# Narrow streams for every product, and a 64-byte lead in the tiles of the normed input

## The chip, the core and the metric

The kernel runs on one core of one Trainium2 chip. The metric is the device time of one execution in microseconds; of the kernel before there are three such times, with a median of 687.1 us. One further execution was taken by the hardware profiler, and everything said of single instructions comes from it. In the profile PE is TensorE's matmul stream and PEld its weight loads, DVE is VectorE, ACT ScalarE, POOL GpSimd, and SP the engine that issues the loads and stores.

## What is computed

Two pre-norm residual layers over 256 tokens of 2048 channels in float32: one of multi-head latent attention (16 heads), one of sliding-window grouped-query attention with sinks (32 query heads, 4 key/value heads), each gated, and a last norm.

```python
for i in range(DEPTH):                      # 2
    h = rmsnorm(x, layer_norm[i])
    if i % 2 == 0:                          # c_q, c_kv, k_rope, gate = split(h @ w_in)
        y, gate = mla_mixer(h, positions, ...)
    else:                                   # q, k, v, gate = split(h @ w_in)
        y, gate = swa_mixer(h, positions, ...)
    x = x + (y * jax.nn.silu(gate)) @ w_out
return rmsnorm(x, final_norm)
```

## The kernel before

The residual stream stays transposed, channels on partitions and the 256 tokens along the free axis, in 16 chunks of 128 channels. A float32 product runs as float32r passes over exact halves: a value is hi + lo, and hi*hi + hi*lo + lo*hi are summed in PSUM. A tile of the normed input (hs, one per chunk of channels) or of the gated mixer output (ys, the same) is [128, 2, 256], the hi half beside the lo half, 2048 bytes a partition. Both families come from the pool const, which hands out tiles one behind the other.

The weights (class Weights, L49 to L96) come in pieces of 128 x 1024. A load on the SP queue fills a raw tile; ACT copies it to the hi half (L89) and DVE subtracts for the lo half (L90). Five raw buffers and four of each half rotate, loads run three pieces ahead of the splits and the splits two ahead of the products. Each piece feeds eight chunks of channels.

`slab` (L254) is the inner product for one piece: half of the channels, for one chunk of 128 outputs. It has two forms. The wide form takes two matmuls a chunk of channels: the lo weights with the 256 hi columns (L266, L269), and the hi weights with all 512 columns of the tile, hi and lo beside each other (L267). Its PSUM bank then holds two sums, which are added afterwards: by `whole` (L271: an ACT copy at L274, a DVE add at L275), or by a second DVE add into the residual (L585, L732). The narrow form (`proj`, L247) takes three matmuls of 256 columns (L250, L251, L252), all into the same 256 columns of PSUM.

The wide form serves layer 0's gates (L551), both output projections (L583, L730) and layer 1's keys (L593); the narrow form layer 1's queries and gates (L635, L646). The latents at the start, the products that bring the latents up to heads (`up`, L453) and the values are narrow in any case.

Program order on each engine is the order in which the code issues. In layer 0, for each of eight pairs of heads: the query's two heads (L482), the previous pair's mix of the values (L466 to L469, whose last product is in plain float32), the query's rope part, the key, the value (L536 to L538), then four gate slabs, with the scores behind the first (L560 to L568) and the float32 transposes of the probabilities (L358, L359) behind the third. In layer 1, for each chunk c: a query half, the transposes, the next scores (L659 to L662), the other query half, a gate half, the values' products (L685, 512 columns wide, and L687), the other gate half. The last two output chunks of layer 1 have a form of their own (L739 to L757).

Of the kernel before, what the change touches and what calls it, by code (L numbers as in the profile page):

```python
"""One MLA layer and one sliding-window GQA layer with sinks, gated, pre-norm, on one core.

The residual stream stays transposed ([channel, token]) from the first load to the last store, so
every projection's result is already the next product's moving operand. Float32 products run as
three float32r passes over exact 12-bit halves (hi*hi + hi*lo + lo*hi, float32 sums in PSUM).
The per-token scale of a norm commutes with the projection behind it and is applied to its result.
"""
# [36 lines left out]
WARM = 2  # L44
MASK_MLA = [(i + 16) % 32 for i in range(32)]
# [3 lines left out]
class Weights:  # L49
    """The weights in the order of use: loads run ahead of the splits, the splits of the products."""  # L50
# [9 lines left out]
    def add(self, ap, width, step=SUB, beside=0):  # L60
        """beside: the halves alternate by that many columns, over the two tiles."""
        for at in range(0, width, step):
            n = min(step, width - at)
            self.pieces.append((ap[:, at:at + n], n, beside))
# [35 lines left out]
def trunk(ctx: ExitStack, tc: tile.TileContext, a: dict):  # L100
# [36 lines left out]
    # the functions' table, before it is waited for  # L137
# [23 lines left out]
    ident = const.tile([P, P], F32, name="ident")  # L161
    make_identity(nc, ident)
    # sums the partitions' two halves, into both
# [9 lines left out]
    # key block | query block: full causal [0 | diag], and window [strictly above | diag]  # L173
# [11 lines left out]
    hs = [const.tile([P, 2, S], F32R, name=f"hs{c}") for c in range(KC)]  # L185
    ys = [const.tile([P, 2, S], F32R, name=f"ys{c}") for c in range(KC)]

# [4 lines left out]
    def split(dst, src):  # L192
        """dst[:, 0] + dst[:, 1] = src, exactly."""
        act.copy(out=dst[:, 0, :], in_=src)
        dve.tensor_tensor(out=dst[:, 1, :], in0=src, in1=dst[:, 0, :].bitcast(F32), op=ALU.subtract)  # L195

    def split_scaled(dst, src, col):
        """The same of src * col, a scale per partition."""
# [4 lines left out]
    class Squares:  # L203
        """The sum over channel chunks of squares, as [128, token]; the rest of the sum is PE's."""
# [14 lines left out]
        def total(self, t):  # L219
            """The sums as a [128 tokens, 2] column, in four columns of a PSUM tile."""  # L220
# [4 lines left out]
    def rsqrt(name, tot, n, times=None):  # L225
        """(tot / n * times ** 2 + eps) ** -0.5 of [128 tokens, 2] columns."""
# [11 lines left out]
    def row(name, col, t):  # L238
        """A [128 tokens, 2] column as a row over the tokens, in every partition; by way of PSUM."""
# [7 lines left out]
    def proj(ps, lhs, rhs, first, last):  # L247
        """ps[n, token] += w.T @ h for one chunk of 128 channels: three passes."""
# [5 lines left out]
    def slab(ps, half, src, wide=True):  # L254
        """ps[n, token] += w.T @ src for half of the channels. Wide: the moving halves share a pass,
        and ps[:, S:] holds the sum with src's lower half."""
        hi, lo = w.next()
        k0 = half * (KC // 2)
        for k in range(k0, k0 + KC // 2):
            n = slice((k - k0) * P, (k - k0 + 1) * P)  # L260
            first, last = k == 0, k == KC - 1
            if not wide:
                proj(ps[:, 0:S], (hi[:, n], lo[:, n]), src[k], first, last)
                continue
            if not first:
                mm(ps[:, 0:S], lhsT=lo[:, n], rhs=src[k][:, 0, :], start=False, stop=False)  # L266
            mm(ps, lhsT=hi[:, n], rhs=src[k].rearrange("p a q -> p (a q)"), start=first, stop=last)  # L267
            if first:
                mm(ps[:, 0:S], lhsT=lo[:, n], rhs=src[k][:, 0, :], start=False, stop=False)  # L269

    def whole(ps):  # L271
        """The sum of a wide pass's two halves."""
        t = work.tile([P, S], F32, tag="wb", name="wb", bufs=1)
        act.copy(out=t, in_=ps[:, S:])  # L274
        dve.tensor_tensor(out=t, in0=ps[:, 0:S], in1=t, op=ALU.add)  # L275
        return t
# [10 lines left out]
    def rope_tables(name, i, pos_f):  # L287
        """cos and signed sin of positions * freq, the angle brought to [-pi, pi]."""
# [25 lines left out]
    def stack_pair(dst, src):  # L314
        """dst[:, 0] = [hi; lo] of src's upper 64 rows, dst[:, 1] = [lo; hi] of its lower 64."""
# [5 lines left out]
    def stack_same(dhi, dlo, src, r):  # L321
        """dhi = [hi; hi], dlo = [lo; lo] of 64 rows of src."""
# [6 lines left out]
    def softmax(ps, j, nm, sm, mask, scale, sink):  # L329
        """exp of one head's scores; -max and the sums, in columns by query block and head of the pair."""  # L330
# [21 lines left out]
    def turn(pair, both):  # L352
        """The pair's probabilities with the keys on partitions, split: key block 0 by head and
        query, then key block 1 by head, for the last queries (there whole, unless both)."""
# [17 lines left out]
    def silu(ps, rB):  # L372
        """silu of a gate chunk: x/2 * (1 + tanh(x/2)), x = ps * rB."""
# [8 lines left out]
    # ================= layer 0 =================  # L382
    # the latents, channel chunk by channel chunk as x arrives: eight output chunks at a time
# [12 lines left out]
    # two output chunks share a bank and one accumulation, which zeros open (and warm the clock)  # L396
# [80 lines left out]
    for g in range(HEADS // 2):  # L477
# [70 lines left out]
        for step in range(4):  # L548
# [3 lines left out]
            if step % 2 == 1:  # L552
                sgs.append(silu(whole(ps), r0B))
# [318 lines left out]
```

## Time and profile before

| | |
|---|---|
| three timed runs | 687.06, 687.10, 687.69 us |
| the profiled execution, first to last instruction | 687.5 us |
| matmuls on PE | 4918 |
| wide matmuls of `slab` (L267) | 480 with ys, 288 with hs |
| narrow passes with hs into pp (L250, L251, L252) | 572 each |
| memory traffic | 113.95 MB read, 2.10 MB written |

The profiled execution's span lies between the fastest and the slowest timed run, so what lies around the span is smaller than what these figures resolve. Stages, by where their first instructions stand: the latents up to about 50 us, layer 0's pairs of heads to 259, its output projection to 349.5, layer 1's keys and values to 373, its loop over chunks to about 590, its output projection to 664, the last two chunks and the final norm to the end.

A window of the profile gives, for a stretch of time, the busy time of each engine with the number of instructions that touch the stretch, the granted TensorE clock (1.00 is full), the DMA engines' share and the rate moved. A group gives line, engine, operation, output and inputs, shapes and count, then the busy time and the mean of one in ns, then the idle time ahead of them and what ended it. Matmuls overlap, and their ends are modelled.

### The profile page before, as it was taken

The page shows a single profiled execution, that of the slowest core. Times are in us where ns is not written, and L with a number is a line of the kernel's source. Part 1 is how long each engine was busy: PE and PEld are TensorE (multiplying, and loading weights), DVE is VectorE, ACT ScalarE, POOL GpSimd, SP SyncE. Part 2 cuts the span into 40 slices and gives each one's busy share as a digit, 9 for nine tenths or more (in the row PEclk, how much of TensorE's full clock was granted, in tenths as well). Part 3 has the DMA queues.
Part 4 walks back from the last instruction along what each step waited for, and adds up shares of the span by engine and source line. Part 5 has one row for each costly group of instructions (what it writes and reads, how often), then busy time and mean ns, then how long its engine had stood idle before and what let it go on. Part 6 is the DMA issues. An engine that isn't in the chain of part 4 may idle for free.

```text
span 687.5 us, 13007 instructions
## 1 busy us (share of the span) xinstructions
PE 672.9 (98%) x4918; PEld 632.1 (92%) x4918; DVE 554.2 (81%) x1133; ACT 435.2 (63%) x871; POOL 64.6 (9%) x72
## 2 busy tenths in 40 slices
PE   8999999999999999999999999999999999999994
PEld 7999899999999998888889999999999999888894
DVE  5887887787788786777768899999998998777764
ACT  6666666766666665444446688787788788444430
POOL 3624000000000000111110000000000000022220
PEclk9999999999999999999999999999999999999997
DMA  8664444554554555555555544544545444555504
GB/s 310 246 217 157 154 157 152 184 161 147 163 166 162 158 180 164 193 186 193 182 185 158 181 157 155 177 155 156 169 146 176 159 151 154 178 190 184 184 32 123
DMA packets 37296, 116.89 MB, mean 170 GB/s; under 512 B 4209, under 2 KB 8945, under 8 KB 37233
## 3 DMA queue, kind: packets, MB, share of 16 engines
q1 hardware_dynamic: 37232, 116.06, 51.6%
q8 instruction: 38, 0.62, 0.4%
q14 instruction: 26, 0.20, 0.1%
HBM read 113.95 MB, written 2.10 MB: 169 GB/s over the span
## 4 chain that ended last, share of the span: by engine, by line
PE 89%; DVE 3%; ACT 3%; POOL 2%; issue 1%; DMA 1%; SPq 0%; DVEq 0%; ACTq 0%; POOLq 0%
PE pp L267 26%; PE pp L266 12%; PE pp L252 11%; PE pp L251 11%; PE pp L250 11%; PE pt L358 2%; ACT whi L89 1%; PE pp L751 1%; PE yp L685 1%; PE pp L537 1%; PE pp L538 1%; PE pp L536 1%; DMA wraw<-in_w_c 1%; DVE wlo L90 1%; PE pp L269 1%
## 5 line engine op out<-in xcount | busy, mean ns | idle before, releaser
L89 ACT CAST whi<-wraw 128x1024 fp32r<-128x1024 f32 (+1 forms) x217 | 223.3, 1030 | 162.7 <-PE pp L267 88.4
L90 DVE TENSOR_TENSOR wlo<-wraw,whi 128x1024 fp32r<-128x1024 f32 (+1 forms) x217 | 260.4, 1202 | 60.8 <-ACT whi L89 58.7
L267 PE MATMUL pp<-ys,whi 128*128 128x512 f32 x480 | 167.7, 397 | 0.0
L252 PE MATMUL pp<-hs,wlo 128*128 128x256 f32 x572 | 159.7, 280 | 1.3 <-DVE wlo L90 1.2
L251 PE MATMUL pp<-hs,whi 128*128 128x256 f32 x572 | 159.6, 279 | 0.5 <-DVE hs L200 0.5
L250 PE MATMUL pp<-hs,whi 128*128 128x256 f32 x572 | 159.5, 279 | 0.2 <-ACT whi L89 0.2
L266 PE MATMUL pp<-ys,wlo 128*128 128x256 f32 x450 | 126.3, 281 | 0.0
L251 PEld LDWEIGHTS pp<-hs,whi 128*128 128x128 f32 x572 | 108.3, 189 | 0.9 <-DVE hs L200 0.9
L252 PEld LDWEIGHTS pp<-hs,wlo 128*128 128x128 f32 x572 | 107.4, 188 | 1.9 <-DVE wlo L90 1.9
L250 PEld LDWEIGHTS pp<-hs,whi 128*128 128x128 f32 x572 | 107.6, 188 | 0.4 <-ACT whi L89 0.4
L216 POOL TENSOR_TENSOR sq_x<-sq_x,sq 128x256 f32<-128x256 f32 x43 | 51.6, 1199 | 581.5 <-ACT sq L215 339.9
L267 PEld LDWEIGHTS pp<-ys,whi 128*128 128x128 f32 x480 | 88.4, 188 | 19.4 <-DVE ys L195 0.2
L267 PE MATMUL pp<-hs,whi 128*128 128x512 f32 x288 | 102.7, 397 | 0.0
L266 PEld LDWEIGHTS pp<-ys,wlo 128*128 128x128 f32 x450 | 84.5, 188 | 1.4
L266 PE MATMUL pp<-hs,wlo 128*128 128x256 f32 x270 | 76.4, 283 | 0.0
L267 PEld LDWEIGHTS pp<-hs,whi 128*128 128x128 f32 x288 | 53.6, 188 | 10.4
L266 PEld LDWEIGHTS pp<-hs,wlo 128*128 128x128 f32 x270 | 50.7, 188 | 0.8
L344 ACT ACTIVATE p<-p,nm 128x128 f32<-128x128 f32 x96 | 42.9, 448 | 12.4 <-DVE nm L340 12.4
L250 PE MATMUL pp<-cq,whi 128*128 128x256 f32 x96 | 27.5, 287 | 0.0
L252 PE MATMUL pp<-cq,wlo 128*128 128x256 f32 x96 | 26.9, 280 | 0.0
L251 PE MATMUL pp<-cq,whi 128*128 128x256 f32 x96 | 26.9, 280 | 0.0
L200 DVE SCALAR_TENSOR_TENSOR hs<-x,gains,hs 128x256 fp32r<-128x256 f32 x32 | 25.0, 792 | 2.1 <-ACT hs L199 2.1
(255 smaller groups left out, 1223.2 us busy)
## 6 DMA issues: line engine op xcount, KB each, us to landing
wraw<-in_w_g SPq DMA_DIRECT2D x64, 512.0 KB, 3.6
wraw<-in_w_o SPq DMA_DIRECT2D x64, 512.0 KB, 3.4
wraw<-in_w_q SPq DMA_DIRECT2D x32, 512.0 KB, 3.6
wraw<-in_w_ukv SPq DMA_DIRECT2D x16, 512.0 KB, 3.6
wraw<-in_w_c SPq DMA_DIRECT2D x15, 512.0 KB, 7.1
wraw<-in_w_uq SPq DMA_DIRECT2D x8, 512.0 KB, 3.6
wraw<-in_w_uq SPq DMA_DIRECT2D x8, 256.0 KB, 2.7
wraw<-in_w_k SPq DMA_DIRECT2D x4, 512.0 KB, 3.3
```

Of the source, the lines that this page charges most:

```text
L89: self.nc.scalar.copy(out=hi, in_=src)
L90: self.nc.vector.tensor_tensor(out=lo, in0=src, in1=hi.bitcast(F32), op=ALU.subtract)
L200: dve.scalar_tensor_tensor(out=dst[:, 1, :], in0=src, scalar=col, in1=dst[:, 0, :].bitcast(F32), op0=ALU.mult, op1=ALU.subtract)
L216: pool.tensor_tensor(out=self.acc, in0=self.acc, in1=t, op=ALU.add)
L250: mm(ps, lhsT=wh, rhs=rhs[:, 0, :], start=first, stop=False)
L251: mm(ps, lhsT=wh, rhs=rhs[:, 1, :], start=False, stop=False)
L252: mm(ps, lhsT=wl, rhs=rhs[:, 0, :], start=False, stop=last)
L266: mm(ps[:, 0:S], lhsT=lo[:, n], rhs=src[k][:, 0, :], start=False, stop=False)
L267: mm(ps, lhsT=hi[:, n], rhs=src[k].rearrange("p a q -> p (a q)"), start=first, stop=last)
L269: mm(ps[:, 0:S], lhsT=lo[:, n], rhs=src[k][:, 0, :], start=False, stop=False)
L344: act.activation(out=p[:, cols], in_=p[:, cols], func=AF.Exp, scale=-1.0, bias=nm[:, c:c + 1], accum_out=sm[:, c:c + 1])
L358: nc.tensor.transpose(t[:, 0, j * S + i * P:j * S + (i + 1) * P], p[:, i * P:(i + 1) * P], ident)
```

## The change

Four edits, and no other (comments and docstrings also go, which moves the line numbers).

1. `slab` keeps only its narrow form; `whole` goes, and so do the second adds into the residual.
2. The values' products of layer 1 with the first key block take two matmuls of 256 columns in place of one of 512.
3. Each hs tile is allocated 16 elements (64 bytes) longer, and its data begin behind these 16. A tile then takes 2112 bytes, so the data of tile c move by 64(c + 1) bytes, and every tile that const and the pools behind it hand out later moves by 1024.
4. Nothing is done to ys, whose tiles keep their form.

```diff
+OFF = 16
...
-    hs = [const.tile([P, 2, S], F32R, name=f"hs{c}") for c in range(KC)]
+    def offset(name):
+        t = const.tile([P, OFF + 2 * S], F32R, name=name)
+        return t[:, OFF:].rearrange("p (a q) -> p a q", a=2)
+
+    hs = [offset(f"hs{c}") for c in range(KC)]
     ys = [const.tile([P, 2, S], F32R, name=f"ys{c}") for c in range(KC)]
...
-    def slab(ps, half, src, wide=True):
+    def slab(ps, half, src):
         hi, lo = w.next()
         k0 = half * (KC // 2)
         for k in range(k0, k0 + KC // 2):
             n = slice((k - k0) * P, (k - k0 + 1) * P)
-            first, last = k == 0, k == KC - 1
-            if not wide:
-                proj(ps[:, 0:S], (hi[:, n], lo[:, n]), src[k], first, last)
-                continue
-            if not first:
-                mm(ps[:, 0:S], lhsT=lo[:, n], rhs=src[k][:, 0, :], start=False, stop=False)
-            mm(ps, lhsT=hi[:, n], rhs=src[k].rearrange("p a q -> p (a q)"), start=first, stop=last)
-            if first:
-                mm(ps[:, 0:S], lhsT=lo[:, n], rhs=src[k][:, 0, :], start=False, stop=False)
-
-    def whole(ps):
-        t = work.tile([P, S], F32, tag="wb", name="wb", bufs=1)
-        act.copy(out=t, in_=ps[:, S:])
-        dve.tensor_tensor(out=t, in0=ps[:, 0:S], in1=t, op=ALU.add)
-        return t
+            proj(ps[:, 0:S], (hi[:, n], lo[:, n]), src[k], k == 0, k == KC - 1)
...
-                sgs.append(silu(whole(ps), r0B))
+                sgs.append(silu(ps[:, 0:S], r0B))
...
         dve.tensor_tensor(out=xc(c), in0=ps[:, 0:S], in1=xc(c), op=ALU.add)
-        dve.tensor_tensor(out=xc(c), in0=ps[:, S:], in1=xc(c), op=ALU.add)
...
-        rope(kf1, whole(kps[c]), cos1R, sin1R, MASK_SWA)
+        rope(kf1, kps[c][:, 0:S], cos1R, sin1R, MASK_SWA)
...
         for n, p in enumerate(pt):
-            mm(yp, lhsT=v0, rhs=p[:, 0:4 * P], start=n == 0, stop=False)
+            for j in range(2):
+                o = slice(j * S, (j + 1) * S)
+                mm(yp[:, o], lhsT=v0, rhs=p[:, o], start=n == 0 and j == 0, stop=False)
```

Two places of PE's order show it. The first is where layer 0 ends: the last pair's mix of the values (yp), and the first chunks of channels of the output projection (pp, from ys). Before:

```order
L468 MATMUL yp<-ptl,vh 128x256
L469 MATMUL yp<-pt_3410,v_3280 128x128
L267 MATMUL pp<-ys_151,whi 128x512
L269 MATMUL pp<-ys_151,wlo 128x256
L266 MATMUL pp<-ys_152,wlo 128x256
L267 MATMUL pp<-ys_152,whi 128x512
L266 MATMUL pp<-ys_153,wlo 128x256
L267 MATMUL pp<-ys_153,whi 128x512
```

Now, with the changed kernel's line numbers (L256 to L258 are `proj`):

```order
L458 MATMUL yp<-ptl,vh 128x256
L459 MATMUL yp<-pt_3613,v_3462 128x128
L256 MATMUL pp<-ys_151,whi 128x256
L257 MATMUL pp<-ys_151,whi 128x256
L258 MATMUL pp<-ys_151,wlo 128x256
L256 MATMUL pp<-ys_152,whi 128x256
L257 MATMUL pp<-ys_152,whi 128x256
L258 MATMUL pp<-ys_152,wlo 128x256
```

Each chunk of channels has three matmuls in place of two, the hi weights come ahead of the lo weights in all of them, and the first slab follows the float32 product directly in both.

The second place is layer 1's loop, between a chunk's two gate halves: the values' products (yp, from the turned probabilities pth and ptl and the values vs). Before:

```order
L252 MATMUL pp<-hs_142,wlo 128x256
L685 MATMUL yp<-pth,vs_4437 128x512
L685 MATMUL yp<-ptl,vs_4437 128x512
L687 MATMUL yp<-pth,vs_4438 128x2x128
L687 MATMUL yp<-ptl,vs_4438 128x2x128
L250 MATMUL pp<-hs_143,whi 128x256
```

Now:

```order
L258 MATMUL pp<-hs_142,wlo 128x256
L676 MATMUL yp<-pth,vs_4911 128x256 x2
L676 MATMUL yp<-ptl,vs_4911 128x256 x2
L678 MATMUL yp<-pth,vs_4912 128x2x128
L678 MATMUL yp<-ptl,vs_4912 128x2x128
L256 MATMUL pp<-hs_143,whi 128x256
```

The gate's passes stand as they did; two products of 512 columns have become four of 256.

More of the change, by code (lines that the diff above doesn't have):

```diff
@@ L634, in query @@
         ps = bank(ps_p, "pp")
-        slab(ps, 0, hs, False)
+        slab(ps, 0, hs)
         yield
-        slab(ps, 1, hs, False)
+        slab(ps, 1, hs)
         qf = work.tile([P, S], F32, tag="ro3", name="ro3")
@@ L645, in gate @@
         ps = bank(ps_p, "pp")
-        slab(ps, 0, hs, False)
+        slab(ps, 0, hs)
         yield
-        slab(ps, 1, hs, False)
+        slab(ps, 1, hs)
         sg_of[c] = silu(ps[:, 0:S], r1B)
@@ L731, in trunk @@
         dve.tensor_tensor(out=xc(c), in0=ps[:, 0:S], in1=xc(c), op=ALU.add)
-        dve.tensor_tensor(out=xc(c), in0=ps[:, S:], in1=xc(c), op=ALU.add)
         sq_x2.add(xc(c))
```

## The prediction

> **What bounds the kernel now.** I read the page's busy time first, then its chain, then its costliest groups.
>
> ```profile
> PE 672.9 (98%) x4918; PEld 632.1 (92%) x4918; DVE 554.2 (81%) x1133; ACT 435.2 (63%) x871; POOL 64.6 (9%) x72
> PE 89%; DVE 3%; ACT 3%; POOL 2%; issue 1%; DMA 1%; SPq 0%; DVEq 0%; ACTq 0%; POOLq 0%
> ...
> L89 ACT CAST whi<-wraw 128x1024 fp32r<-128x1024 f32 (+1 forms) x217 | 223.3, 1030 | 162.7 <-PE pp L267 88.4
> L267 PE MATMUL pp<-ys,whi 128*128 128x512 f32 x480 | 167.7, 397 | 0.0
> L252 PE MATMUL pp<-hs,wlo 128*128 128x256 f32 x572 | 159.7, 280 | 1.3 <-DVE wlo L90 1.2
> ```
>
> PE is busy for 98% of the span and holds 89% of the chain. The weights' splits wait for PE (162.7 us idle before L89, 88.4 of it until L267 releases a buffer), not PE for them: L267 has no idle time, L252 1.3 us. So TensorE's own pace sets the time, and the question is what one streamed column costs. The mean of one matmul does not say it, because a matmul's end is modelled and overlaps the next one's start. I therefore took stretches that begin with the first pass of a slab (eight channel chunks) and end where the next work starts:
>
> ```profile
> core 0: us, PE busy (x), PEclk, DMA share, GB/s
> 91.29:94.01 2.72, 2.72 (x27) 1.00 0.46 142
> 405.79:408.51 2.72, 2.72 (x27) 1.00 0.50 178
> 85.92:88.75 2.83, 2.83 (x25) 1.00 0.57 185
> 409.20:412.02 2.82, 2.82 (x26) 1.00 0.54 186
> 104.23:107.05 2.82, 2.82 (x18) 1.00 0.47 166
> 276.19:281.83 5.64, 5.64 (x33) 1.00 0.58 190
> ...
> 395.37:408.51 13.14, 13.14 (x115) 1.00 0.49 161
> ```
>
> (The x counts up to three neighbours whose ends reach in.) In order: the key's two heads from ck, 24 narrow passes; layer 1's first gate half, 24; the query's two heads from cq, 24; the second gate half of the same chunk, 24; a layer 0 gate slab, 8 wide pairs; an output chunk of layer 0, two slabs of 8 wide pairs; and one whole round of layer 1's loop. Every slab streams 24 x 256 = 6144 columns, wide or narrow, and the granted clock is 1.00 in all. Yet there are two paces: 2.72 us (113 ns for 256 columns) and 2.82 us (117.5 ns). The wide slabs show the slow one; the narrow ones show both, with identical instructions:
>
> ```profile
> L252 PE MATMUL pp<-hs,wlo 128*128 128x256 f32 x9 | 2.5, 276 | 0.0
> L251 PE MATMUL pp<-hs,whi 128*128 128x256 f32 x9 | 2.5, 276 | 0.0
> L250 PE MATMUL pp<-hs,whi 128*128 128x256 f32 x8 | 2.2, 276 | 0.0
> ...
> L251 PE MATMUL pp<-hs,whi 128*128 128x256 f32 x8 | 2.2, 281 | 0.0
> L252 PE MATMUL pp<-hs,wlo 128*128 128x256 f32 x8 | 2.2, 281 | 0.0
> L250 PE MATMUL pp<-hs,whi 128*128 128x256 f32 x8 | 2.2, 281 | 0.0
> ```
>
> These are the two gate halves, 405.80 to 408.48 and 409.21 to 412.00: 276 ns a pass in the one, 281 in the other. Between them stand the values' products, two of them 512 wide. So I read two **rhythms**, and a narrow slab keeps the one it enters with. What leaves a narrow slab in the fast one is a fresh start at the first pass of a channel chunk, as behind the values' float32 product in layer 0:
>
> ```profile
> 89.68 0.38 PE L469 MATMUL yp<-pt,v 128*128 128x128 f32 x2
> 89.82 0.36 PE L250 MATMUL pp<-cq,whi 128*128 128x256 f32 x1
> 90.02 0.28 PE L251 MATMUL pp<-cq,whi 128*128 128x256 f32 x1
> ...
> 90.61 0.28 PE L250 MATMUL pp<-cq,whi 128*128 128x256 f32 x1
> 90.72 0.28 PE L251 MATMUL pp<-cq,whi 128*128 128x256 f32 x1
> 90.83 0.28 PE L252 MATMUL pp<-cq,wlo 128*128 128x256 f32 x1
> 90.95 0.28 PE L250 MATMUL pp<-cq,whi 128*128 128x256 f32 x1
> ```
>
> From 90.61 to 90.95 three passes take 0.34 us, and the key behind them (91.29 above) goes on at 2.72 until the next wide slab.
>
> **The change, part by part.** The span is 687.5 against a median of 687.1: I sum against the span and take 0.4 off at the end.
>
> Narrow in place of wide: 768 pairs become triples of the same columns. The slabs are 32 in layer 0's output projection, 28 in layer 1's (its last two chunks are as before), 32 gate slabs of layer 0 and 4 of layer 1's keys: 96. At the slow rhythm nothing is won; at the fast one each wins 2.82 - 2.72 = 0.10, together 9.6 us. The entries speak for the fast one: layer 0's output projection now follows the same float32 product as the row at 89.82, and two of a group's four gate slabs follow the narrow value products or the float32 transposes.
>
> Values in halves: the four half products stream the same columns, and nothing 512 wide stands in layer 1's loop any more. If it was this that upset the rhythm, the second gate half and the query half after it go from 2.82 to 2.72: 14 chunks x 2 x 0.10 = 2.8 us.
>
> The query's two heads in layer 0 (85.92, at 2.83) follow a gate slab that is no longer wide: 7 groups x 0.11 = 0.8 us.
>
> Given back: after a restart a few passes run slow (90.02 to 90.61 is 0.59 us for five, 0.02 more than at the fast rhythm). At most four times a group in layer 0's gates, that is 32 x 0.02 = 0.6 us.
>
> The Trainium skill's page "TensorE: Matmul & The Clock Gate" (Back-to-back issue gap) speaks against the change: each matmul costs its columns at 2.4 GHz and about 2.5 ns, so 768 more matmuls would cost 1.9 us and no slab would be won. Here 256 columns take 113 or 117.5 ns, not the 109 of that rule, so I do not sum by it.
>
> ACT and DVE lose work:
>
> ```profile
> L274 ACT COPY wb<-pp x18: 352/374/375, 80.3 to 364.8; 128x256 f32<-128x256 f32 x18
> L275 DVE TENSOR_TENSOR wb<-pp,wb x18: 418/425/426, 80.7 to 365.5; 128x256 f32<-128x256 f32 x18
> L585 DVE TENSOR_TENSOR x<-pp,x x16: 424/424/425, 265.6 to 350.2; 128x256 f32<-128x256 f32 x16
> ...
> 393.00:577.00 184.00, 184.00 (x1569) 182.85 (x1568) 170.33 (x439) 143.84 (x337) 0.00 (x0) 1.00 0.49 161
> ```
>
> Eighteen foldings and 30 second adds go, about 27 us of busy time. (The last row's pairs are PE, PEld, DVE, ACT and POOL in layer 1's loop.) All of it lies under PE, which is not seen idle in the stages concerned, so I cost it at nothing; a gain of up to half a microsecond at layer 1's start is not counted. What is late next is DVE in layer 1's loop: 170.33 of 184.00 us. There no DVE work goes, and PE's loop would shrink by 2.8 to 181.2, still 11 us above DVE's.
>
> The offset: an hs tile grows from 2048 to 2112 bytes a partition, so tile c's data moves by 64(c + 1) bytes while weights and ys all move by 1024. Against a weight slice (a multiple of 512 bytes into its tile), the odd tiles keep their distance modulo 128 and the even ones shift by 64. No long run of such passes is in the trace. 2400 passes stream hs in the slabs (768 layer 0 gates, 96 keys, 1536 queries and gates), half of them from even tiles. The nearest rows are single passes at which stream and weights change their tiles:
>
> ```profile
> L252 PE MATMUL pp<-cq,wlo 128*128 128x256 f32 x1 | 0.3, 285 | 0.0
> L250 PE MATMUL pp<-hs,whi 128*128 128x256 f32 x1 | 0.3, 286 | 0.0
> ```
>
> The first is the last query pass before the mix (88.6), the second layer 1's first query pass (372.98); they take 9 to 10 ns more than 276. From below, no narrow row is under 276, so I allow no gain beyond the fast rhythm except as a small chance. So the even passes cost 0 to 1200 x 9 = 10.8 us. I take 0, since 276 is also what hs, cq and ck passes show in whole slabs. The Trainium skill's page "SBUF — State Buffer" (Who interferes with whom) says the same: TensorE's two read ports are independent and wait for nobody, which makes the offset worth 0; that two rhythms exist at one clock shows that something else is missing from it.
>
> Sum: 9.6 + 2.8 + 0.8 - 0.6 = 12.6 us; 687.5 - 12.6 = 674.9, and less 0.4 it is **674.5**.
>
> **The rivals.**
> *The shifted tiles hold half of the passes back.* If the even tiles' passes run at the slow rhythm, 1200 x 4.2 ns = 5.0 us come back: 679.5. For it: the distance is all that differs. Against: the rows above show no tie between distance and rhythm.
> *All hs slabs fall into the slow rhythm*, since every second tile upsets it: 2400 x 4.2 = 10.1 us back, 684.6. Only ys gains.
> *The rhythm is not the width's doing.* Wide or narrow, everything stays as it is; the extra matmul of a triple then costs what separates two slow narrow slabs (2.82 and 2.83) from a wide chunk (5.64): 0.01 us in 16 channel chunks, 0.5 us in 768. 687.6. Against it: the row at 89.82 and the gate halves. By the 2.5 ns of the Trainium skill's page "TensorE: Matmul & The Clock Gate" (Back-to-back issue gap) it would be 689.0.
> *Slower: the even tiles collide with the weight load.* Each even pass pays the 9 ns of the 285 row, and the odd passes behind them the slow rhythm's 4.2: 1200 x 9 + 1200 x 4.2 = 15.8 us, 690.3. It decides from 12.6 / 2400 = 5.3 ns a pass on, just above the slow rhythm.
> *The even tiles stream better* than any row shows, by as much as the two known rhythms lie apart: 1200 x 4.2 = 5.0 us more, 669.5.
>
> **How the numbers follow.** Forecast 50% (672 to 678); half held back 17%; all hs slow 8%; rhythm not of the width 8%; collision 12%; better 5%. A measurement of this kernel can tell about 0.2%, 1.4 us. Faster is 50 + 17 + 8 + 5 = 80%, no change 8%, slower 12%. The range 669 to 686.5 takes in all the faster cases and leaves out the last 20%; the likeliest's own is 672 to 678.
>
> **What would show it.** In the changed profile an output chunk should take 5.44 us, not 5.64; passes of ys and hs should average 276 ns, not 281; layer 1's loop 12.94 us a chunk (13.14 now). The wait of ACT's split for PE should shorten. If odd and even hs tiles differ in their passes, the offset is at work; if ys passes read 281, the rhythm is not the width's. PE idle time for wlo in layer 1's loop would mean that DVE has become the bound.

## The result, and the profile after

| | before | after |
|---|---|---|
| median of the runs | 687.39 us (687.06 to 687.95, 4 runs) | 692.26 us (691.49 to 692.65, 4 runs) |
| profiled execution, span | 687.5 us | 690.3 us |
| that execution, timed | not known | 692.13 us |

The ratio is 1.0064, with a 95% interval of 1.0049 to 1.0078: the change costs 0.64%. The forecast was 674.5 us, and its range ended at 686.5.

First the page of the changed kernel: busy times, then groups (line, engine, operation, tiles, shape and count | busy us, mean ns of one | idle time ahead and what ended it).

```profile
PE 676.2 (98%) x5718; PEld 672.1 (97%) x5718; DVE 534.9 (77%) x1085; ACT 428.2 (62%) x853; POOL 63.9 (9%) x72
...
L90 ACT CAST whi<-wraw 128x1024 fp32r<-128x1024 f32 (+1 forms) x217 | 223.2, 1030 | 176.5 <-PE pp L257 150.1
L256 PE MATMUL pp<-hs,whi 128*128 128x256 f32 x860 | 242.3, 282 | 0.9 <-ACT whi L90 0.9
L257 PE MATMUL pp<-ys,whi 128*128 128x256 f32 x480 | 133.7, 278 | 0.1
```

PE is the bound as before, and its idle time ahead of these groups is at most 0.9 us. The wait of ACT's split for PE has grown to 176.5 us, where the prediction had it shorten. The passes of ys have a mean of 278 ns, those of hs 282. Only hs has the lead, but the 278 is itself a mixture: 276 ns in the first output projection and 281 in the last, with the same instructions.

Next, windows: stretch, length and PE busy time with its count, granted clock, DMA share and rate. The five stretches of each kernel are layer 0 from its first query pass, its output projection, layer 1's keys and values, the loop over chunks, and the last output projection up to the last matmul. Before:

```profile
58.55:259.18 200.63, 199.88 (x1464) 1.00 0.50 162
259.18:349.51 90.33, 90.33 (x515) 1.00 0.56 184
349.51:372.98 23.47, 23.47 (x170) 1.00 0.48 159
372.98:584.28 211.30, 210.82 (x1792) 1.00 0.50 163
584.28:679.12 94.84, 93.10 (x563) 1.00 0.43 142
```

After:

```profile
58.04:260.70 202.66, 201.84 (x1721) 1.00 0.49 161
260.70:347.85 87.15, 87.15 (x772) 1.00 0.58 190
347.85:371.40 23.55, 23.55 (x202) 1.00 0.54 168
371.40:586.88 215.48, 215.15 (x1823) 1.00 0.48 159
586.88:682.29 95.41, 93.41 (x789) 1.00 0.43 141
```

The first output projection, which streams ys, gains 3.18 us. Layer 0's heads (hs in the gates) lose 2.03, the loop (hs in queries and gates) 4.18, the last projection 0.57. With the keys' 0.08, and 0.51 and 0.37 won ahead of the first row and behind the last matmul, this is the 2.8 us between the spans. The clock is 1.00 in every row.

Shorter windows of the same trace: one output chunk of layer 0; a gate slab of layer 0; two slabs of layer 1's loop, one right behind the other (the second half of a query, the first of a gate), of 24 narrow passes each; the whole round that begins with them.

```profile
277.13:282.57 5.44, 5.44 (x51) 1.00 0.60 198
103.97:106.81 2.84, 2.84 (x27) 1.00 0.30 110
402.01:404.85 2.84, 2.84 (x27) 1.00 0.72 208
404.85:407.69 2.84, 2.84 (x27) 1.00 0.43 170
402.01:415.43 13.42, 13.42 (x117) 1.00 0.50 160
```

The output chunk takes the forecast 5.44 us. The three slabs of hs take 2.84, longer than either of the two paces of before (2.72 and 2.82), and the loop's round 13.42 where 12.94 was forecast and 13.14 stood. From start to start, the loop's hs passes behind its first two queries (some 1430, stalls apart) lie 118.3 ns apart, where before they had 115.6.

In the runs below, the profiled execution's time is 1.7 to 1.9 us longer than its span (3.2 in run 2). So what lies around the span is not as small as it seemed ahead of the prediction: the profiled execution of before (687.5) was, by this estimate, one of about 689.3 us, at the upper end of its runs (687.32 to 689.51 over 25 later ones). That would account for spans that differ by 2.8 us where the medians differ by 4.9.

### The profile page after: what moved, and what is told of

It reads as the page before. It is cut to its first block, busy times and chain, and to the rows that moved or that the text cites. A ratio compares the mean times of both kernels' runs of the same rounds, so it can differ in the third digit from the quotient of the medians.

```text
span 690.3 us, 14550 instructions
## 1 busy us (share of the span) xinstructions
PE 676.2 (98%) x5718; PEld 672.1 (97%) x5718; DVE 534.9 (77%) x1085; ACT 428.2 (62%) x853; POOL 63.9 (9%) x72
## 4 chain that ended last, share of the span: by engine, by line
PE 88%; DVE 4%; ACT 3%; issue 2%; POOL 1%; DMA 1%; SPq 0%; POOLq 0%; DVEq 0%; ACTq 0%
PE pp L257 24%; PE pp L258 24%; PE pp L256 24%; PE pt L348 1%; ACT whi L90 1%; DVE wlo L91 1%; PE yp L676 1%; PE pp L526 1%; PE pp L528 1%; PE pp L527 1%; DMA wraw<-in_w_c 1%; PE pp L741 1%; PE pt L349 1%; PE sc L648 1%; PE sc L610 1%
## 5 line engine op out<-in xcount | busy, mean ns | idle before, releaser
L90 ACT CAST whi<-wraw 128x1024 fp32r<-128x1024 f32 (+1 forms) x217 | 223.2, 1030 | 176.5 <-PE pp L257 150.1
L256 PE MATMUL pp<-hs,whi 128*128 128x256 f32 x860 | 242.3, 282 | 0.9 <-ACT whi L90 0.9
L258 PE MATMUL pp<-hs,wlo 128*128 128x256 f32 x860 | 242.0, 282 | 0.7 <-DVE wlo L91 0.5
L257 PE MATMUL pp<-hs,whi 128*128 128x256 f32 x860 | 241.9, 281 | 0.3 <-DVE hs L206 0.3
L258 PEld LDWEIGHTS pp<-hs,wlo 128*128 128x128 f32 x860 | 162.6, 189 | 1.3 <-DVE wlo L91 1.3
L256 PEld LDWEIGHTS pp<-hs,whi 128*128 128x128 f32 x860 | 162.1, 189 | 1.1 <-ACT whi L90 1.1
L257 PEld LDWEIGHTS pp<-hs,whi 128*128 128x128 f32 x860 | 162.0, 188 | 0.5 <-DVE hs L206 0.5
L257 PE MATMUL pp<-ys,whi 128*128 128x256 f32 x480 | 133.7, 278 | 0.1
L256 PE MATMUL pp<-ys,whi 128*128 128x256 f32 x480 | 133.6, 278 | 0.0
L258 PE MATMUL pp<-ys,wlo 128*128 128x256 f32 x480 | 133.5, 278 | 0.0
L256 PEld LDWEIGHTS pp<-ys,whi 128*128 128x128 f32 x480 | 91.0, 190 | 0.0
L257 PEld LDWEIGHTS pp<-ys,whi 128*128 128x128 f32 x480 | 90.1, 188 | 0.3 <-DVE ys L201 0.3
L258 PEld LDWEIGHTS pp<-ys,wlo 128*128 128x128 f32 x480 | 90.1, 188 | 0.0
L256 PE MATMUL pp<-cq,whi 128*128 128x256 f32 x96 | 27.3, 284 | 0.0
L258 PE MATMUL pp<-cq,wlo 128*128 128x256 f32 x96 | 26.7, 278 | 0.0
L309 DVE TENSOR_TENSOR qs<-ro,qs 64x256 fp32r<-64x256 f32 x48 | 20.2, 420 | 7.7 <-ACT qs L308 6.7
L308 ACT CAST qs<-ro 64x256 fp32r<-64x256 f32 x48 | 19.2, 400 | 8.3 <-DVE ro L302 7.7
```

What stands on the lines that cost most here:

```text
L90: self.nc.scalar.copy(out=hi, in_=src)
L256: mm(ps, lhsT=wh, rhs=rhs[:, 0, :], start=first, stop=False)
L257: mm(ps, lhsT=wh, rhs=rhs[:, 1, :], start=False, stop=False)
L258: mm(ps, lhsT=wl, rhs=rhs[:, 0, :], start=False, stop=last)
L308: act.copy(out=dst[r, j, :], in_=src[r, :])
L309: dve.tensor_tensor(out=dst[o, j, :], in0=src[r, :], in1=dst[r, j, :].bitcast(F32), op=ALU.subtract)
```

## The experiments

In this section the **distance** is the address of a streamed tile within a partition less that of the weight slice, modulo 256 bytes. It is worked out from the addresses that the program's tiles are given. Before the change it is 192 for hs, ys, cq and ck alike. In the changed kernel ys stays at 192, while hs tiles go through 0, 64, 128 and 192 in turn. The weight slices themselves lie at 160 or 32 modulo 256, which is 32 modulo 128 in every kernel here. So where the runs below vary the distance, they vary the tile's own address modulo 128 with it, and none of them tells the two apart. A time in brackets is the range of the runs.

**1. Narrow, without the lead.** `OFF = 0`, all else as in the changed kernel.

```diff
-OFF = 16
+OFF = 0
```

> The changed kernel without the 64-byte lead: every product narrow, hs tiles where they were before. Theory A (the lead upsets the rhythm, the narrow form does not): hs passes fall back from 118.3 to about 113.5 ns, ck passes too; with some 2700 hs passes outside the latents that is 2700 x 4.6 = 12 us less, a span of 677 to 680, and 678 to 682 timed. Theory B (the extra matmul and weight load of the narrow form is what holds hs back): the passes stay at 118 and the span at 689 to 691. The changed kernel's timed runs lie 1.8 us above their spans; if that goes with the 800 more matmuls (C), it is there again.

Measured 684.7 us (680.1 to 689.02, ten runs), ratio 0.9959 [0.9934, 0.9985]. The windows of the profiled execution, which at 680.1 us was the fastest of the ten, by the same five stretches:

```profile
56.59:256.29 199.70, 198.65 (x1721) 1.00 0.50 163
256.29:343.44 87.15, 87.15 (x772) 1.00 0.59 190
343.44:366.73 23.29, 23.29 (x203) 1.00 0.52 170
366.73:577.86 211.13, 210.64 (x1822) 1.00 0.50 162
577.86:670.06 92.20, 90.20 (x789) 1.00 0.45 146
```

So the lead alone turns a gain into a loss: 7.6 us between the medians (7.2 by the two ratios). Narrowing itself gains, but about a quarter of what was forecast, and the runs spread over 9 us where before spread over 2. The loop (211.13) is no faster than before (211.30). Two slabs of it show why:

```profile
396.80:399.52 2.72, 2.72 (x26) 1.00 0.66 214
402.92:405.75 2.83, 2.83 (x26) 1.00 0.51 181
```

Between them stand the values' products, 256 wide now. They still leave the slow pace behind them.

**2. The shift alone, wide slabs.** The kernel before; the even hs tiles come first, behind 64 bytes of padding, and the odd ones behind 64 more. The distance is 128 for the even tiles and 192 for the odd.

```diff
-    hs = [const.tile([P, 2, S], F32R, name=f"hs{c}") for c in range(KC)]
+    hs = [None] * KC
+    for first_c in range(2):
+        const.tile([P, 16], F32, name=f"lead{first_c}")
+        for c in range(first_c, KC, 2):
+            hs[c] = const.tile([P, 2, S], F32R, name=f"hs{c}")
```

> The kernel before, wide slabs kept, with the even hs tiles shifted by 64 bytes against the weight slices and the odd ones not, as in the changed kernel (the even tiles are allocated behind one 64-byte tile, the odd ones behind a second, since 64 bytes for every tile leave no room). Theory A: layer 1's narrow hs passes go from 115.6 to 118.3 ns, 1442 x 2.7 = 3.9 us, the gates' wide ones from 116.7 to 118 or more, 0.8 us: 691 to 693. Theory B: 687 to 688, layer 1's passes at 115.6.

Measured 693.43 us (692.6 to 694.46), ratio 1.0069 [1.0052, 1.0086]. Its loop, narrow in this kernel too:

```profile
373.67:588.27 214.60, 214.23 (x1791) 1.00 0.48 160
```

That is 3.3 us more than before. The wide gate slabs of layer 0 keep their pace (116.8 ns for 256 columns, 116.7 before). The shift costs without any narrowing, and it costs the narrow passes; the wide ones are slow already.

**3. All hs tiles shifted alike.** Narrow; all 16 hs tiles at distance 128, so that nothing changes from tile to tile.

```diff
-    hs = [offset(f"hs{c}") for c in range(KC)]
+    const.tile([P, 16], F32, name="lead0")
+    hs = [const.tile([P, 2, S], F32R, name=f"hs{c}") for c in range(KC)]
+    const.tile([P, 16], F32, name="lead1")
```

> The changed kernel with all sixteen hs tiles shifted by the same 64 bytes against weights and ys, none left at the old distance. If it is the alternation from tile to tile that upsets the rhythm (A1), hs passes run at 113.5 ns and the span is that of the kernel without the lead, 677 to 680. If it is the distance itself (A2: stream and weight load in step modulo 128 bytes), all hs passes take 118.5 or more, twice the shifted ones: 690 to 697. Theory B: 690.

Measured 693.69 us (691.76 to 695.06), ratio 1.0075 [1.0055, 1.0094]. Windows: layer 0's output projection, the loop, and two slabs of it.

```profile
261.70:348.85 87.15, 87.15 (x771) 1.00 0.59 190
372.54:589.50 216.96, 216.64 (x1822) 1.00 0.48 157
403.21:406.06 2.85, 2.85 (x26) 1.00 0.68 216
409.62:412.50 2.88, 2.88 (x27) 1.00 0.55 182
```

The place of the tiles costs even where they do not alternate: at 128 throughout, no slab of hs is fast, while ys at 192 is.

**4. The values 512 wide again.** As run 1, with the values' products as before the change.

```diff
-            for j in range(2):
-                o = slice(j * S, (j + 1) * S)
-                mm(yp[:, o], lhsT=v0, rhs=p[:, o], start=n == 0 and j == 0, stop=False)
+            mm(yp, lhsT=v0, rhs=p[:, 0:4 * P], start=n == 0, stop=False)
```

> Narrow slabs, no lead, but layer 1's value products 512 columns wide as before. If a 512-column stream is what throws a narrow slab out of the fast rhythm, the second gate half and the next query half of 14 chunks run at 117.6 ns again: 28 x 0.10 = 2.8 us more than without the lead and with halves. If not, the same time within 0.5 us.

Measured 687.26 us (682.86 to 688.02), ratio 0.9976 [0.9959, 0.9992]. Output projection and loop:

```profile
256.91:347.45 90.54, 90.54 (x772) 1.00 0.56 184
370.96:582.54 211.58, 211.20 (x1791) 1.00 0.50 161
```

The loop is within 0.5 us of run 1: halving the values bought it next to nothing. The output projection, whose instructions are the same in runs 1 and 4, took 87.15 there and 90.54 here. A whole stage can thus run in either rhythm. That could account for run 1's spread of 9 us; only one of its ten executions has a trace.

**5 to 7. ys shifted; hs shifted by 32 and by 96 bytes.** Narrow, padding as in run 3 in other places and sizes. Run 5 puts ys at 128, and hs at 64, because the padding moves the weights too; run 6 hs at 96; run 7 hs at 160; ys is at 192 in the last two. The edit shown is that of run 5, against run 3.

```diff
-    const.tile([P, 16], F32, name="lead0")
     hs = [const.tile([P, 2, S], F32R, name=f"hs{c}") for c in range(KC)]
-    const.tile([P, 16], F32, name="lead1")
+    const.tile([P, 16], F32, name="lead0")
     ys = [const.tile([P, 2, S], F32R, name=f"ys{c}") for c in range(KC)]
+    const.tile([P, 16], F32, name="lead1")
```

> Narrow products everywhere, no lead; the 16 ys tiles (not hs) lie 64 bytes further, so that in the two output projections stream and weight slice are 0 apart modulo 128 bytes, as the even hs tiles were in the changed kernel. Theory (the distance costs, whatever the tile): ys passes start 118 to 119 ns apart in both output projections, never 113.4, so 96 us becomes 90.9 us each (87.0 at the fast rhythm); hs passes stay as in the narrow kernel without lead (113.9 in layer 0's gates, 115.6 in layer 1's loop). Time 687 to 690. Rival (something of the hs tiles alone, their writers or their place behind the inputs): ys passes at 113.4 or 117.7, time as without lead, 680 to 689, median near 684.7.

> Narrow products everywhere; all hs tiles 32 bytes further, ys where they were: hs streams then lie 96 bytes from the weight slices modulo 128 instead of 64. Theory 1 (only distance 0 costs): hs passes as without a lead, 113.4 where they are fast and 117.7 where slow, layer 1's loop at 115.6; median 684 to 686. Theory 2 (what counts is how far the 64-byte halves overlap): half the price, hs passes never at 113.4 but 115 to 118 everywhere, time 687 to 691. Theory 3 (64 bytes is itself an unlucky distance and the flips come from it): hs passes at 113.4 throughout, time 677 to 681.

> As the run with 32 bytes, but the hs tiles 96 bytes further: the distance to the weight slices modulo 128 is 32 bytes instead of 64. The three theories give the same as for 32 bytes: only distance 0 costs, median 684 to 686 with layer 1's loop at 115.6; overlap counts, 687 to 691 with no pass at 113.4; 64 is itself unlucky, 677 to 681. If 32 and 96 differ from each other, the sign of the distance matters (which of the two accesses runs ahead).

Measured 694.19 (693.62 to 694.97, ratio 1.0083 [1.0068, 1.0098]), 696.03 (692.5 to 696.62, 1.0099 [1.0071, 1.0126]) and 687.99 us (686.95 to 688.89, 0.9993 [0.9983, 1.0003]). From run 5 the output projection and two hs slabs, then one hs slab each of runs 6 and 7:

```profile
259.63:350.85 91.22, 91.22 (x771) 1.00 0.55 181
376.67:379.39 2.72, 2.72 (x26) 1.00 0.83 261
404.18:407.00 2.82, 2.82 (x26) 1.00 0.68 218
```
```profile
400.19:403.05 2.86, 2.86 (x26) 1.00 0.57 173
```
```profile
400.98:403.79 2.81, 2.81 (x26) 1.00 0.67 208
```

Distance 128 costs ys what it cost hs: 91.22 us, longer than either pace of the stage. It is no property of the hs tiles. Run 5 was slower than its forecast of 687 to 690, as hs at 64 ran slow in the loop from its first scores on (117.8 ns), though not everywhere: 64 still has both paces (2.72 and 2.82). At 96 and 160 the loop's passes lie 119.8 and 117.9 ns apart and the fast pace does not appear. The three theories on 32 and 96 bytes had one price for both; the middle one, 687 to 691, holds for run 7, and none foresaw run 6.

**8. The values ahead of the transposes.** As run 1; in layer 1's loop the values' products of a chunk move from the middle of its gate to directly ahead of the next chunk's transposes.

```diff
+        if c > 0:
+            values(c - 1)
+            gated(c - 1)
         pt_of[c] = turn(p_of.pop(c), True)
...
-        if c + 2 < KC:
-            values(c)
         next(gt)
-        if c + 2 >= KC:
-            values(c)
-        gated(c)
+    values(KC - 1)
+    gated(KC - 1)
```

> Narrow products everywhere, no lead; in layer 1's loop the products with the values of chunk c stand directly ahead of the six transposes of chunk c+1 instead of between the gate's two halves. Theory (the values' products leave the slow rhythm behind them, the transposes and scores behind them the fast one): all hs passes of the loop at 113.4, so 48 of 96 passes of 14 chunks save 4.3 ns each, 2.9 us: loop 115.6 to 113.4 on average, median 681 to 682 where the narrow kernel without lead had 684.7. Rival (the rhythm changes at a fixed count or place of the loop, not behind the values): half of the passes of a chunk stay at 117.8, time as without lead, near 684.7.

Measured **681.93 us** (681.88 to 682.14), ratio 0.9905 [0.989, 0.992], as forecast. The loop, one round of it, and one of the round's slabs:

```profile
370.97:579.93 208.96, 208.58 (x1823) 1.00 0.51 165
414.40:427.32 12.92, 12.92 (x116) 1.00 0.52 166
417.12:419.84 2.72, 2.72 (x26) 1.00 0.35 130
```

The prediction's round (12.94) is there, bought by the order of the products and not by their width. From 401 us on, every slab of the loop has the fast pace.

**9 and 10. The order of run 8, with leads.** Run 9 has the change's lead of 64 bytes in every hs tile. Run 10 has 128 bytes in every second tile: the same memory, and tiles that lie at 64 and 192 in pairs.

```diff
-    hs = [offset(f"hs{c}") for c in range(KC)]
+    hs = [offset(f"hs{c}", 32 if c % 2 == 0 else 0) for c in range(KC)]
```

> The changed kernel itself (narrow products, 64-byte lead in every hs tile) with the values' products of layer 1 directly ahead of the transposes, as in the run that held the loop at 113.4 ns a pass. So the lead is the one difference to that run. Theory (a stream that is not 64 bytes from the weights modulo 128 has no fast rhythm): hs passes at 118 to 119 everywhere, 1442 loop passes x 4.7 = 6.8 us and about 1100 passes of layer 0, the keys and the latents x 4.4 = 4.8 us more than without the lead: 681.9 + 9 to 12 = 691 to 694, no better than the changed kernel. Rival (the lead hurt only by meeting the values' products' slow phase): the loop goes to 113.4 to 115 and the time below 687.

> As the run with the values ahead of the transposes, but every second hs tile begins 128 bytes into its allocation: the same memory and the same kind of lead as in the change, and all streams stay 64 bytes from the weights modulo 128. Theory (the distance modulo 128, not the lead): loop near 113.6 and the time within 3 us of 681.9. Rival 1 (it is the lead or the uneven spacing of the tiles that costs): loop 118, time 691 to 694. Rival 2 (the period is 256 bytes; neighbouring tiles now differ by 128): loop between, 116 to 118, time 686 to 691.

Measured 688.85 (688.46 to 689.39, ratio 1.0006 [0.9997, 1.0015]) and 688.57 us (686.26 to 690.5, 0.9998 [0.998, 1.0016]). Loop and last projection of run 9, and the loop of run 10:

```profile
371.41:586.86 215.45, 215.22 (x1823) 1.00 0.49 160
586.86:678.79 91.93, 90.16 (x789) 1.00 0.43 143
```
```profile
371.93:584.32 212.39, 212.03 (x1822) 1.00 0.50 163
```

With the lead the loop takes 215.45 us in this order and 215.48 in the change's: where no slab is fast, the order is worth nothing. Between runs 8 and 9 the lead costs 6.9 us, less than the forecast 9 to 12. Run 9 beats the changed kernel by 3.4 because its last projection is fast (91.93 against 95.41). Run 10 speaks against the theory that only the distance modulo 128 counts: its loop loses 3.4 us to run 8's, and not evenly. In its trace the passes of tiles 0, 1, 4, 5 and so on (distance 64) start about 117.8 ns apart, those of tiles 3, 7, 11 and 15 (the second of a pair at 192) 113.6 to 113.9, those of the first of such a pair 115.6 to 115.8. So the pace changes within a slab where neighbouring tiles differ by 128 bytes. Whether it is the jump or the place at 64 that does it is not shown; in run 5, at 64 throughout, some slabs are fast.

**11. Wide slabs, the values ahead of the transposes.** The kernel before, with the edit of run 8.

> The kernel before, wide slabs and 512-wide values as they are, with the values' products directly ahead of the transposes. Theory (half of the loop is slow because of where the values' products stand, not of their width): loop 115.6 to 113.4, 14 chunks x 48 passes x 4.3 ns = 2.9 us, 688 to 685. Theory of the prediction (a 512-wide product leaves the slow rhythm and nothing else does): behind the 512-wide products now come the transposes, so it would give the same here; the two differ in that the narrow values did not help where they stood. Rival (only all-narrow kernels can be fast over a whole chunk): loop stays at 115.5, 688.

Measured 685.82 us (685.38 to 686.19), ratio 0.9959 [0.9944, 0.9974]. Its loop:

```profile
372.44:580.86 208.42, 207.98 (x1791) 1.00 0.50 167
```

The loop gains 2.9 us with 512-wide values in it: their place counts, not their width. Between this and run 8 lie 3.9 us more, from narrow slabs and values.

**12. Transposes ahead of the output projection.** As run 8, with six transposes of a constant tile, unread, behind layer 0's last mix.

```diff
     mixes()
+    t = ps_t.tile([P, 2, 512], F32, tag="pt", name="pt")
+    for i in range(6):
+        nc.tensor.transpose(t[:, 0, 0:P], mask_c[:, P:], ident)
```

> As the run with the values ahead of the transposes, with six transposes of a constant tile (their result is not read) between layer 0's last mix and the first output projection, which ran at 117.8 in that run. Theory (six transposes lead into the fast rhythm): the output projection goes to 113.4, 768 x 4.4 = 3.4 us less 0.7 for the transposes: 679 to 679.5. Rival (what follows depends on the instructions right behind as well, here none of the scores): it stays at 117.8 and the time is 682.6.

Measured 682.87 us in the median of eleven runs, near the rival's 682.6, but from 678.08 to 691.4: four took 688.4 to 691.4, and the ratio of the other seven is 0.9903 [0.9886, 0.992]. The profiled execution took 691.37. Its first output projection and its loop:

```profile
257.15:347.69 90.54, 90.54 (x772) 1.00 0.55 181
371.19:586.32 215.13, 214.88 (x1822) 1.00 0.49 160
```

In this execution the transposes did not make the projection fast; what they did in the others is open. The loop says more. Its instructions are those of run 8, and hs lies at 192, yet from 391 us on every slab has the slow pace (117.8 ns a pass), and the loop takes 6.2 us more than run 8's at the same granted clock. So behind its first rounds the order of run 8 keeps a pace; it does not choose which.

**13. The values' products once more.** As run 8, with the six products repeated, unread, between the halves of chunk 7's gate (`again` holds the matmuls of `values`).

```diff
+        if c == 7:
+            again(c)
         next(gt)
```

> As the run with the values ahead of the transposes (no lead), with the six products of the values done once more, unread, between the two halves of the gate of chunk 7 alone. Theory of flips (a group of products that streams other tiles flips the rhythm; values, and transposes with scores, each flip it once, so the values ahead of the transposes keep it): every hs slab from there to the loop's end runs at 117.8 where it ran at 113.4: 0.7 us for the six, and 8 chunks x 96 + 48 less what has no query, about 600 to 650 passes x 4.4 ns = 2.7 us: 685.2 to 685.6 where that run had 681.9; in the profile 113.4 before chunk 7's second gate half and 117.8 behind it, across all later transposes. Rival (the prediction's fresh start: transposes lead into the fast rhythm whatever was before): one or two slabs slow, 681.9 + 0.7 + 0.2 = 682.8. If the loop is slow from its first chunk, the run decides nothing.

Measured 681.67 us (681.41 to 682.03), ratio 0.9906 [0.989, 0.9923]: not the forecast 685.2 to 685.6. But the trace shows the flip exactly. In order: the loop's round before the extra products, the slab right ahead of them (they stand from 480.12 to 480.80), the slab right behind them, the next slab behind transposes and scores, a round, and a slab four rounds later.

```profile
461.76:474.68 12.92, 12.92 (x116) 1.00 0.50 164
477.40:480.12 2.72, 2.72 (x26) 1.00 0.31 122
480.80:483.63 2.83, 2.83 (x26) 1.00 0.44 140
488.54:491.36 2.82, 2.82 (x26) 1.00 0.65 200
488.54:501.92 13.38, 13.38 (x116) 1.00 0.47 151
547.74:550.56 2.82, 2.82 (x26) 1.00 0.31 97
```

One group of six products turned the rest of the loop slow, across all the transposes behind it. A restart by the transposes would have ended it by 488.54. One reading fits the rounds of runs 1, 8, 11, 12 and 13 from the third on: the values' products flip the pace, the transposes and scores flip it once more, and the two directly behind each other leave it as it was. It is a reading, and no run tested the transposes' share alone. In the first two rounds it fails: run 8's slabs go from slow to fast at 401.48 and run 13's at 410.08, behind the same groups that leave the pace alone later, and run 12's do not. The loop as a whole, and the output projection ahead of it:

```profile
366.48:579.43 212.95, 212.59 (x1828) 1.00 0.50 162
256.04:343.19 87.15, 87.15 (x772) 1.00 0.60 190
```

The loop loses 4.0 us to run 8's (forecast 3.4). The time of this execution doesn't show it, since layer 0's output projection, untouched, was fast here (87.15; 90.53 in run 8).

**14. Six products ahead of the output projection.** As run 8, with six unread float32r products of layer 0's last probabilities and values behind the last mix.

```diff
     mixes()
+    t = ps_t.tile([P, 2, 512], F32, tag="pt", name="pt")
+    for i in range(6):
+        mm(t[:, 0, 0:S], lhsT=vh[:, i % 2 * P:(i % 2 + 1) * P], rhs=pth[:, i % 2 * S:(i % 2 + 1) * S],
+           start=True, stop=True)
```

> As the run with the values ahead of the transposes (no lead), with six float32r products of 256 columns from layer 0's last probabilities and values, unread, between the last mix and the first output projection, which ran at 117.8 in that run. Theory of flips: the group turns the output projection and the keys behind it to 113.4: 768 x 4.4 = 3.4 us and about 0.8 for the keys less 0.7 for the six: 678.4 to 679.3. Rival (six products change nothing, or what decides lies in the entry from the fp32 product alone): 682.6. Where they also turn the loop's entry to the slow rhythm the loop loses 1442 x 4.3 = 6.2 us: 684.6.

Measured 683.14 us (681.75 to 685.34), ratio 0.9929 [0.9907, 0.9951]; the profiled execution's projection:

```profile
257.70:348.16 90.46, 90.46 (x771) 1.00 0.56 181
```

It is slow, and none of the four runs shows the forecast 678.4 to 679.3. That does not tell whether the group flips the pace: run 13 and run 8 have the same instructions up to this stage, and took 87.15 and 90.53 us in it with nothing inserted.

## Why the prediction was wrong

**The bound and the two rhythms** were read rightly. PE's pace sets the time in every run; narrow slabs take 2.72 or 2.82 us, and in run 8 (distance 192, values directly ahead of the transposes) the loop's round takes 12.92 us where 12.94 was forecast. Run 12 has the same loop and ran it slow, so that even with these parts right the forecast round is one of two.

**"I take 0 for the offset"** is the step that decided. It was taken because 276 ns stood in whole slabs of hs, cq and ck; but all of these lay at one distance, so their agreement could say nothing of another. The lead costs 7.6 us without and 6.9 with the better order, inside the bounds of 0 to 10.8, and the text took their lower end. Without the lead the median of 684.7 would have lain in the stated range, but by the range's width: only about a quarter of the forecast gain is there. The mechanism comes nearest to the rival in which all hs slabs fall into the slow rhythm (4.2 ns a pass): 118.3 ns is 5.0 above the fast 113.3. Its time of 684.6 was too low, because the other terms failed as well. The colliding tiles' 690.3 lies nearer, by another price: even and odd tiles hardly differ (means by tile from 117.2 to 119.2 ns in the loop), and no tile's passes pay 9 ns in the mean. The Trainium skill's page "SBUF — State Buffer" (Who interferes with whom), by which the two read ports wait for nobody, gave 0 for the lead in the prediction; the lead cost some 7 us, and no run shows whether a port is what it costs.

**"What leaves a narrow slab in the fast rhythm is a fresh start"** was wrong. Run 13 shows that transposes do not restart it: a group of products in between flips the rhythm, and the slabs keep what they got. The row behind the float32 product on which this rested was one such change. The trace of before already held both outcomes. These are two stretches of twelve narrow hs passes at its start, the first behind a wait of 1.00 us for the weights, the second behind one of 0.22 us for hs, with nothing 512 wide between them:

```profile
35.97:37.33 1.36, 1.36 (x14) 1.00 0.71 292
42.06:43.47 1.41, 1.41 (x14) 1.00 0.73 183
```

That is 113.3 and 117.8 ns a pass: a new start gave the fast pace once and the slow one once, and no width was needed for the slow one. In run 1 and in the changed kernel the same place leaves the key and the value products of layer 0 slow (117.9 ns, 113.3 before). Of the 9.6 us for 96 slabs, the first output projection gave its 3.2 (3.18 measured). The last gave none in the changed kernel and 2.6 in run 1 (94.84 to 92.20). Layer 0's gates and query, 3.4 by the sum, are worth 0.9 for the whole of layer 0 in run 1 (200.63 to 199.70): the keys and values there give back some 0.2 us in most pairs of heads.

**"Values in halves", 2.8 us,** was put on the wrong cause. Runs 1, 4 and 11 show that the rhythm changes behind them, or does not, by their place and not by their width. Run 8 finds the gain by moving them.

**The work that goes from ACT and DVE** was priced at nothing, and no row shows a gain from it. **The step from span to median** (0.4 off) was wrong by its sign: 1.8 us lies outside the span, and the profiled execution was a long one.

**Open** is what sets the rhythm where an output projection or the loop begins: 87.15 or 90.53 us, and 208.96 or 215.13, with the same instructions. The gain of 3.18 us in the changed kernel's first output projection is therefore partly luck. Open is also whether the lead acts by the distance to the weights or by the tile's own address. Why the two rhythms exist was not tried.

## What to carry to other kernels

A duration in a profile can belong to a state of the machine and not to an instruction: where the same instructions show two paces, ask what changes the pace, and test it by one inserted group, before summing as if every slab had the better one. Do not move a streamed tile without a measurement, even by 64 bytes; equal readings at one place are no evidence on another. And where a gain depends on such a state, order the work so that a fast pace is kept: order and narrow form together gave 0.95% in run 8, and each alone 0.4% (runs 11 and 1). Take several executions before trusting such a gain, since run 12 shows that the same order keeps the slow pace as well.

## What the runs showed of the hardware

- A float32r pass of 256 columns at a granted clock of 1.00 has two steady paces, 113.3 and 117.7 to 117.8 ns. The Trainium skill's page "TensorE: Matmul & The Clock Gate" (Back-to-back issue gap) gives one for a matmul by itself, columns at 2.4 GHz and 2.5 ns, which would be an estimated 109 ns; no stretch of these passes shows it.
- The pace depends on where the streamed tile lies. With its distance to the weight slice at 192 or 64 bytes modulo 256 both paces occur; at 96, 128 and 160 only 117 to 120 ns as means of a slab. That the distance and not the tile's own address counts is not shown.
- Where neighbouring tiles differ by 128 bytes, the pace changes within a slab, 117.8 to 113.6 ns and back (run 10). Six products of other tiles changed it for the rest of a loop, 2.72 to 2.82 us a slab (run 13).
- The kernel before, whose loop is half slow by its order, repeats within 2 us. The all-narrow kernel without a lead spreads over 9 us, and whole stages were seen in either rhythm: 87.15 and 90.54 us (runs 1 and 4).
- Time less span does not grow with the instructions: 1.8 us with the 13009 of run 11 as with the 14550 of the changed kernel.
